# A last RMSNorm whose sums are spread by a matrix of ones, and other banks for the first output tiles, in a hybrid decoder layer

## The chip, the cores and the metric

The kernel runs on one core of a Trainium2 chip. The time is the device time of one execution in microseconds, and a run is judged by the median of several executions. A profiled execution of the kernel before gives the span, the busy times of the engines, and the order of every instruction. TensorE is called PE in the profile (PEld are its weight loads), VectorE is DVE, ScalarE is ACT, GpSimd is POOL, and SP is the engine that issues most of the transfers.

## The reference

The layer takes `x` of 1 x 1024 x 1024 (tokens by channels, f32). Cut to what matters here:

```python
h = rmsnorm(x, norm1_w)
proj = h @ w_in                      # q, k, v, z of mixer A; gates; q, k, v of mixer B
o_a = (rmsnorm(gated_delta_rule(...), gdn_norm_w) * silu(z))      # 4 heads of 128
o_b = dilated_attention(qb, kb, vb)                               # 8 heads of 64
x = x + concat([o_a, o_b]) @ w_out
h = rmsnorm(x, norm2_w)
u = causal_dwconv(h @ w_up, ffn_conv_w)
x = x + (silu(gate) * up) @ w_down
return rmsnorm(x, final_norm_w)      # x * rsqrt(mean(x * x over channels) + 1e-6) * w
```

The last line is the norm that the change rewrites. The product with `w_out` is the output projection, whose banks it exchanges.

## The kernel before

Everything is held transposed: channels on the 128 partitions, tokens along the free dimension. A row of 1024 channels is so eight tiles of 128 partitions, and a norm over channels is a sum over partitions and over eight tiles. Products are made three times with parts of f32 (high by high, low by high, high by low; `mm3`), at the rate of fp32r; a few small ones are plain f32 products.

Python code writes the program. A planner (`Weave`) runs the stages as streams and fixes the order on TensorE; `need` makes a stream wait, in the planner's own model of time, until a tile is ready. On the other engines the framework's scheduler sets the order from the dependencies and from its own simulated timeline; `after(a, b)` adds an order by hand, `keep` chains instructions in the order written. `defer` puts pieces of VectorE's work into a queue from which `background` takes them.

PSUM has eight banks, in four pairs with tags: `hf` (the projection), `asc` (attention's scores and their transposes), `ch` and `atr`. `bank(tag)` takes the next one of a pair, which must have been read out by those who used it last.

The output projection (`out_proj`, line 1328) makes eight tiles of 128 output channels, each in two halves of 512 tokens, summed over k = 0 to 7 (four heads of mixer A, four pairs of heads of mixer B). The first two tiles (`MORDER[0]`, `MORDER[1]`) are made side by side while the last heads are still being split into high and low parts (`ohi`, `olo`): for each k that is done, first the two halves of the one tile, then those of the other. Their banks are taken on line 1358: `hf` for the first, `asc` for the second. All later tiles take `hf` (line 1369). Just before, the stream `dense` has made the last tile of z in the `hf` banks; VectorE reads it out into `xr`. VectorE also finishes the last attention group (`oT`), the gate (`zz`, `og`), and the low parts of the heads (`olo`).

At the end (`mlp_down`, line 1865) the last product is made in pieces. The eight tiles of the result, `x1h[0]` to `x1h[7]`, are complete for the second half of the tokens first; of the first half, the left 256 tokens and then the right 256 are finished. For the last piece the squares of `x1h[4]` and `x1h[5]` are added into `rstdB` with the others, and those of `x1h[6]` and `x1h[7]` are kept alone (`squares`). Then `final_norm(0, right, ("hf", "ch"), more=squares)`, line 1924, does this:

- TensorE multiplies each 128-token block of the three square tiles, as weights, with one column of ones: the sums come out with tokens on partitions, two numbers per partition (`ss`).
- ScalarE takes the root, VectorE the reciprocal, of those two numbers (`rs`).
- Four transposes of `rs`, spread along its free dimension, put one copy of the result on all partitions into a bank (`pb`), and a second copy into another bank (`pb_`).
- ScalarE copies the second one to SBUF (`pbs`), and GpSimd multiplies `x1h[2]` and `x1h[3]` by it; ScalarE has scaled these two by the norm's weight `fw` before.
- VectorE scales the other six tiles by `fw` and `pb` in one instruction each (line 1840), and each tile is stored when it is done, by SP's queue or ScalarE's.

The left part's eight scalings (`outs`) are put around this by hand, lines 1921 to 1923:

```python
        after(outs[1], last["sum"], "the last norm waits for it")
        after(outs[1], adds[2, right.start], "the last norm waits for it")
        after(outs[5], adds[3, right.start], "the last norm waits for it")
```

`adds[3, ...]` is VectorE's addition of the last product to its tile.

Of the kernel before, what the change touches and what calls it, by code (L numbers as in the profile page):

```python
# [7 lines left out]
F32 = mybir.dt.float32  # L8
F32R = mybir.dt.float32r
AF = mybir.ActivationFunctionType  # L10
OP = mybir.AluOpType
# [4 lines left out]
P = 128  # L16
# [134 lines left out]
def hybrid_layer(tc, I, out):  # L151
# [3 lines left out]
    ve = Engine(wv, nc.vector, "vector", 0.07, 0.00105)  # L155
    ac = Engine(wv, nc.scalar, "scalar", 0.12, 0.00085)
# [3 lines left out]
    po_ = Engine(wv, nc.gpsimd, "gpsimd", 0.15, 0.0021)  # L160
    sy = Engine(wv, nc.sync, "sync", 0.05, 0.00142, 2.2)
# [3 lines left out]
    sa = Engine(wv, nc.scalar, "sync", 0.05, 0.00142, 2.2)  # L165
# [4 lines left out]
    sp = es.enter_context(tc.tile_pool(name="sp", bufs=1))  # L170
# [3 lines left out]
    def tile_(pool, shape, dt, name, tag, bufs):  # L174
        return wv.slot(pool.tile(list(shape), dt, name=name, tag=tag, bufs=bufs), tag, bufs)
# [12 lines left out]
    def const(name, shape, src=None):  # L188
        t = cp.tile(list(shape), F32, name=name)
        if src is not None:  # L190
            sy.dma_start(t, src)
        return t
# [3 lines left out]
    def after(inst, anchor, reason="keeps a slot free until it is needed"):  # L196
        tc.add_manual_dep(inst.ins, anchor.ins.name, order, reason=reason)
# [44 lines left out]
    def mm(dst, lhs, rhs, us, start=True, stop=True, **kw):  # L242
        tc.stamp_issue_order_token(nc.tensor.matmul(dst, lhs, rhs, start=start, stop=stop, **kw).ins, TOKEN)  # L243
        wv.product(us, dst, lhs, rhs)

    def tp(dst, src):
        tc.stamp_issue_order_token(nc.tensor.transpose(dst, src, ident).ins, TOKEN)  # L247
        wv.product(0.11, dst, src)
# [45 lines left out]
    eps = const("eps", [P, 1])  # L294
# [26 lines left out]
    def bank(tag, name="ps"):  # L321
        return tile_(pp_, (P, 512), F32, name, tag, 2)
# [40 lines left out]
    for k in range(KT):  # L363
# [11 lines left out]
        if k == 0:  # L375
            sy.dma_start(wst[:, 0, :], I["w0"][0, :, 0])
            for h in range(2):
# [8 lines left out]
                                         op0=OP.mult, op1=OP.subtract)  # L386
# [3 lines left out]
        else:  # L390
            if k % 2 == 0:
                sy.dma_start(wst, I["w0"][k // 2])
            parts = [half(0), half(1)] if k == 1 else [slice(0, S)]
# [14 lines left out]


    ident = const("ident", [P, P], I["ident"])  # L410
    ones = const("ones", [P, 8])
    ve.memset(ones, 1.0)
    tri = tile_(sp, [P, P], F32, "tri", "r0", 1)
    sy.dma_start(tri, I["tri"])
# [41 lines left out]
    rstdB = const("rstdB", [P, S])  # L456
# [834 lines left out]
    last = {}  # L1291
# [34 lines left out]
    fw = const("fw", [P, KT], I["fw"])  # L1326

    def out_proj():
        yield from wv.until("dense")
        kept, pieces[:] = pieces[:], []  # L1330
        made = first_out + [wk(I["wo"][MORDER[1]], None, 4)]
        pieces.extend(kept)
        ws, lows = [t[:2] for t in made], [t[2:] for t in made]
        yield from wv.until("last group")
        yield from wv.until("residual")
        pts, third = {}, []
        todo = [(k, j) for k in range(8) for j in range(2)]
        while todo:

            now = [a for a in todo if ("ot", a[0]) in wv.done and (a[1] == 0 or "attention" in wv.done)]  # L1340
            if not now:
                yield 0.3
                continue
            k, j = now[0]
            todo.remove(now[0])
            m, w = MORDER[j], ws[j]
            last["products"] = True
            for low in lows[j]:
                flush(low)
            if k == H and not third:  # L1350

                third.extend(A(nm, "qa", F32R) for nm in ("whi", "wlo"))
                raw = raw_weight(I["wo"][MORDER[2]])
                ac.activation(third[0], raw, AF.Copy)
                defer(*[(third[1], lambda c=c: ve.tensor_tensor(third[1][:, c], raw[:, c], third[0][:, c].bitcast(F32),
                                                                op=OP.subtract), [third[0]]) for c in quarters])
            if m not in pts:
                pts[m] = [bank(("hf", "asc")[j]) for _ in range(2)]
            for h in range(2):
                yield wv.need(pts[m][h], *w, *ots[k])  # L1360
                mm3(pts[m][h], [t[:, k, :] for t in w], [t[:, half(h)] for t in ots[k]], k == 0, k == 7)
        wv.done.add("firsts")
        for j, m in enumerate(MORDER):
            w = ws.pop(0)
            for h in range(2):
                if j > 1:
                    if j == 2:
                        flush(third[1])
                    pt = bank("hf")
                    yield wv.need(pt, *w)  # L1370
                    for k in range(8):
                        mm3(pt, [t[:, k, :] for t in w], [t[:, half(h)] for t in ots[k]], k == 0, k == 7)
                        yield 0.0
                else:
                    pt = pts[m][h]
                ve.tensor_tensor(x1[m][:, half(h)], x1[m][:, half(h)], pt, op=OP.add)
            if j + 2 < 8:
                ws.append(wk(I["wo"][MORDER[j + 2]]) if j else
                          [t.rearrange("p (k m) -> p k m", k=KT) for t in third])
                load_residual(MORDER[j + 2])  # L1380
            elif j == 6:
                up_first()
                wv.done.add("last weights")
            residual(m)
        wv.done.add("proj")
# [224 lines left out]
    x1h = {}  # L1610
# [160 lines left out]
    def part(m, hh, sl):  # L1771
        return slice(512 * hh + sl.start, 512 * hh + sl.stop)
# [22 lines left out]
            if turn:  # L1795
                keep("vector", inst)

    def final_norm(hh, sl, tags, between=None, more=()):
        n_ = (sl.stop - sl.start) // P
        ss = bank(tags[0])  # L1800
        o = 512 * hh + sl.start
        parts = [rstdB[:, o:o + n_ * P]] + list(more)
        for i, t in enumerate(parts):
            for c in range(n_):
                mm(ss[:, c:c + 1], t[:, c * P:(c + 1) * P], ones[:, :1], 0.215, i == 0 and c == 0,
                   i == len(parts) - 1, skip_group_check=True)
        rs = tile_(sp, [P, 4], F32, "rs3", "rs3", 2)
        if more:
            ac.activation(rs[:, :n_], ss[:, :n_], AF.Sqrt, scale=1.0 / 1024, bias=eps)
            ve.reciprocal(rs[:, :n_], rs[:, :n_])  # L1810
        else:
            inst = ve.tensor_scalar(rs[:, :n_], ss[:, :n_], 1.0 / 1024, EPS, op0=OP.mult, op1=OP.add)
            rsqrt(rs[:, :n_], rs[:, :n_], n_)
        if hh:

            keep("vector", inst)
            rp, rs = rs, tile_(sp, [P, 4], F32, "rs3", "rs3", 2)
            keep("vector", ve.tensor_copy(rs, rp))
        elif between is not None:
            rp, rs = rs, tile_(sp, [P, 4], F32, "rs3", "rs3", 2)  # L1820
            last["mean"] = ve.tensor_copy(rs[:, :n_], rp[:, :n_])
        if between is not None:
            between()
        pb = bank(tags[1])
        for c in range(n_):
            tp(pb[:, c * P:(c + 1) * P], rs[:, c:c + 1].to_broadcast([P, P]))
        insts = []
        if more:

            pb_ = bank(tags[0])  # L1830
            for c in range(n_):
                tp(pb_[:, c * P:(c + 1) * P], rs[:, c:c + 1].to_broadcast([P, P]))
            ps_ = tile_(sp, [P, 256], F32, "pbs", "t2", 2)
            ac.activation(ps_, pb_[:, :n_ * P], AF.Copy)
            for m in (2, 3):
                x = x1h[m][:, part(m, hh, sl)]
                po_.tensor_tensor(x, x, ps_, op=OP.mult)
        for m in (0, 1, 4, 5, 6, 7) if more else range(8):
            x = x1h[m][:, part(m, hh, sl)]
            insts.append(ve.scalar_tensor_tensor(x, x, fw[:, m:m + 1], pb[:, :sl.stop - sl.start], op0=OP.mult, op1=OP.mult))  # L1840
            (sa if more and m in (1, 6) else sy).dma_start(out[m * P:(m + 1) * P, part(m, hh, sl)], x)
            if more and m in (4, 6):

                m = 2 if m == 4 else 3
                sa.dma_start(out[m * P:(m + 1) * P, part(m, hh, sl)], x1h[m][:, part(m, hh, sl)])
        return insts

    def square(m, hh=0):
# [16 lines left out]
    def mlp_down():  # L1865
# [3 lines left out]
        pb = [bank(t, "dw") for t in ("hf", "ch") for _ in range(2)]  # L1869
# [15 lines left out]
        for n, (stage, j) in enumerate(STEPS):  # L1885
# [5 lines left out]
            if (stage, j) == (3, HT - LAST - 2):  # L1891
                outs = final_norm(1, whole, ("hf", "ch"), lambda: down_step(stage, j))
# [7 lines left out]
        adds = {}  # L1900
# [19 lines left out]

        after(outs[1], last["sum"], "the last norm waits for it")
        after(outs[1], adds[2, right.start], "the last norm waits for it")
        after(outs[5], adds[3, right.start], "the last norm waits for it")
        final_norm(0, right, ("hf", "ch"), more=squares)

    wv.add(0, norms())
    wv.add(1, gates())
# [73 lines left out]
```

## Time and profile before

| What | Value |
|---|---|
| median of 3 runs | 1181.21 us (1180.98 to 1181.97) |
| profiled execution, its own time | 1181.01 us |
| its span | 1179.2 us |
| PE busy | 1170.6 us (99%) |
| DVE busy | 948.1 us (80%) |
| ACT busy | 555.5 us (47%) |
| POOL busy | 54.2 us (5%) |
| mean granted clock of TensorE | 0.998 |

The span runs from the first to the last instruction of the execution; the time has a little more around it. In the rows of the timeline the first number is the start in us from the span's start, the second the duration of the row (of all its instructions together, where it ends in x2 or more), then engine, line, operation, output <- inputs, and forms; in brackets stands how long the engine was idle before, and who ended that. In the rows of groups the numbers behind the count are the busy time in us and the mean of one in ns. Most instructions carry the line of a helper (L142 for VectorE, ScalarE and GpSimd, L243 for products, L247 for transposes), so the names of the tiles tell them apart.

### The profile page before, as it was taken

The page shows a single profiled execution, that of the slowest core. Times are in us where ns is not written, and L with a number is a line of the kernel's source. Part 1 is how long each engine was busy: PE and PEld are TensorE (multiplying, and loading weights), DVE is VectorE, ACT ScalarE, POOL GpSimd, SP SyncE. Part 2 cuts the span into 40 slices and gives each one's busy share as a digit, 9 for nine tenths or more (in the row PEclk, how much of TensorE's full clock was granted, in tenths as well). Part 3 has the DMA queues.
Part 4 walks back from the last instruction along what each step waited for, and adds up shares of the span by engine and source line. Part 5 has one row for each costly group of instructions (what it writes and reads, how often), then busy time and mean ns, then how long its engine had stood idle before and what let it go on. Part 6 is the DMA issues. An engine that isn't in the chain of part 4 may idle for free.

```text
span 1179.2 us, 18158 instructions
## 1 busy us (share of the span) xinstructions
PE 1170.6 (99%) x6958; PEld 967.0 (82%) x6958; DVE 948.1 (80%) x1559; ACT 555.5 (47%) x1000; POOL 54.2 (5%) x46
## 2 busy tenths in 40 slices
PE   9999999999999999999999999999999999999997
PEld 7888888898777778888888888888888888888887
DVE  8676997464566677768999898888989889998987
ACT  7473433333334444655545454444444453546452
POOL 0122001003200000000000000000000000000001
PEclk9999999999999999999999999999999999999999
DMA  7424566838564315532231222223131494457734
GB/s 241 109 82 148 146 166 182 260 100 252 183 193 136 126 38 171 196 126 96 83 107 57 104 75 87 93 69 108 54 107 54 150 388 168 131 178 226 233 98 160
DMA packets 122103, 167.48 MB, mean 142 GB/s; under 512 B 55776, under 2 KB 70944, under 8 KB 122016
## 3 DMA queue, kind: packets, MB, share of 16 engines
q1 hardware_dynamic: 121296, 165.80, 43.8%
q8 instruction: 54, 0.88, 0.3%
q10 hardware_dynamic: 720, 0.53, 0.1%
q14 instruction: 33, 0.27, 0.1%
HBM read 126.09 MB, written 40.21 MB: 141 GB/s over the span
## 4 chain that ended last, share of the span: by engine, by line
PE 99%; DVE 1%; ACT 0%; issue 0%; DVEq 0%; ACTq 0%
PE ps L243 48%; PE pa L243 20%; PE dw L243 18%; PE pc L243 10%; PE ps L252 1%; PE ps L247 1%; DVE x1h L142 0%; PE warm L243 0%; PE pd L243 0%; DVE wke L144 0%; ACT w L144 0%; DVE aqkv L142 0%; DVE xr L142 0%; ACT sq L142 0%; DVEq L1997 0%
## 5 line engine op out<-in xcount | busy, mean ns | idle before, releaser
L243 PE MATMUL dw<-pr 128*128 128x512 f32 (+1 forms) x984 | 211.4, 377 | 0.0
L243 PEld LDWEIGHTS dw<-pr 128*128 128x128 f32 x984 | 176.7, 188 | 33.6
L243 PE MATMUL ps<-xhi,whi 128*128 128x512 f32 x448 | 177.0, 409 | 0.0
L243 PE MATMUL ps<-xhi,wlo 128*128 128x512 f32 x448 | 169.5, 391 | 0.0
L243 PE MATMUL ps<-xlo,whi 128*128 128x512 f32 x448 | 169.1, 391 | 0.0
L243 PE MATMUL pa<-T,pair 128*128 128x512 f32 x528 | 126.9, 389 | 0.0
L243 PEld LDWEIGHTS pa<-T,pair 128*128 128x128 f32 x528 | 99.2, 188 | 20.6
L243 PEld LDWEIGHTS ps<-xhi,whi 128*128 128x128 f32 x448 | 84.1, 188 | 18.7 <-issue 2.1
L243 PEld LDWEIGHTS ps<-xhi,wlo 128*128 128x128 f32 x448 | 84.0, 188 | 18.8 <-issue 0.6
L243 PEld LDWEIGHTS ps<-xlo,whi 128*128 128x128 f32 x448 | 84.2, 189 | 15.4 <-DVE xlo L142 0.4
L142 ACT ACTIVATE u<-pa 128x512 f32<-128x512 f32 x44 | 26.4, 599 | 114.4 <-PE pa L243 114.3
L142 DVE SCALAR_TENSOR_TENSOR y<-xu,fcw,y 128x1023 f32<-128x1023 f32 (+1 forms) x44 | 56.4, 1281 | 22.1 <-ACT y L142 22.0
L142 ACT ACTIVATE pr<-wd 128x1024 fp32r<-128x1024 f32 x33 | 35.0, 1061 | 73.6 <-DVE wd L142 38.6
L243 PE MATMUL pa<-B,A 128*128 128x512 f32 x264 | 63.5, 390 | 0.0
L243 PE MATMUL pc<-B,pair 128*128 128x512 f32 x264 | 63.4, 389 | 0.0
L243 PE MATMUL pc<-T,S 128*128 128x512 f32 x264 | 63.4, 389 | 0.0
L243 PE MATMUL pa<-T,S 128*128 128x512 f32 x264 | 63.4, 389 | 0.0
L142 DVE TENSOR_TENSOR wst<-wst 128x512 f32<-128x512 f32 x88 | 60.4, 686 | 0.8
L243 PE MATMUL ps<-B,pair 128*128 128x512 f32 x252 | 60.5, 389 | 0.0
L144 ACT ACTIVATE sm<-sm,mx 128x128 f32<-128x128 f32 (+7 forms) x64 | 35.4, 555 | 51.6 <-DVE mx L144 51.6
L142 DVE TENSOR_TENSOR wlo<-wst,whi 128x256 fp32r<-128x256 f32 (+3 forms) x74 | 47.9, 676 | 13.9 <-ACT whi L142 13.8
L243 PEld LDWEIGHTS pa<-T,S 128*128 128x128 f32 x264 | 49.6, 188 | 10.3
(245 smaller groups left out, 2155.1 us busy)
## 6 DMA issues: line engine op xcount, KB each, us to landing
wst<-in_wu SPq DMA_DIRECT2D x44, 512.0 KB
wd<-in_wd SPq DMA_DIRECT2D x44, 512.0 KB
wst<-in_wi SPq DMA_DIRECT2D x25, 512.0 KB
upark<-y SPq DMA_DIRECT2D x22, 512.0 KB
r<-upark SPq DMA_DIRECT2D x22, 512.0 KB
wa<-in_wd SPq DMA_DIRECT2D x22, 256.0 KB
apark<-aqkv SPq DMA_DIRECT2D x8, 512.0 KB
wst<-in_wo SPq DMA_DIRECT2D x8, 512.0 KB
```

The source lines that it names most:

```text
L142: return getattr(eng, op)(*a, **kw)
L144: inst = getattr(eng, op)(*a, **kw)
L243: tc.stamp_issue_order_token(nc.tensor.matmul(dst, lhs, rhs, start=start, stop=stop, **kw).ins, TOKEN)
L247: tc.stamp_issue_order_token(nc.tensor.transpose(dst, src, ident).ins, TOKEN)
L252: tc.stamp_issue_order_token(nc.tensor.transpose(dst, src[rows], ident[rows, rows]).ins, TOKEN)
```

## The change

The last piece's norm gets a function of its own, `last_norm`. It multiplies the three square tiles, now as the moving operand of 256 columns, with a 128 x 128 matrix of ones as weights: each product puts the sum over partitions on every partition, and the three accumulate in one bank (`ss`, 128 x 256). ScalarE takes the root of all 256 columns into SBUF (`root`), VectorE writes the reciprocal into another bank (`pb`), ScalarE copies that to SBUF for GpSimd (`by`), and the scalings and stores follow as before. The transposes, the small `rs` and the second bank are gone from it; `final_norm` loses the branches for `more`. The tile `ones` grows from 8 to 128 columns. One more of the left part's scalings is put behind the last addition (`outs[4]` in place of `outs[5]`).

In `out_proj`, the first tile takes the `asc` banks and the second the `hf` banks; the third tile takes `asc`, and the others `hf`.

```diff
-    ones = const("ones", [P, 8])
+    ones = const("ones", [P, P])
     ve.memset(ones, 1.0)
...
             if m not in pts:
-                pts[m] = [bank(("hf", "asc")[j]) for _ in range(2)]
+                pts[m] = [bank(("asc", "hf")[j]) for _ in range(2)]
...
-                    pt = bank("hf")
+                    pt = bank("asc" if j == 2 else "hf")
...
-    def final_norm(hh, sl, tags, between=None, more=()):
+    def last_norm(sl, tags, more):
+        n = sl.stop - sl.start
+        ss, pb = bank(tags[0])[:, :n], bank(tags[1])[:, :n]
+        for i, t in enumerate([rstdB[:, sl]] + more):
+            mm(ss, ones, t, 0.43, i == 0, i == len(more))
+        root, by = [tile_(sp, [P, 256], F32, nm, "t2", 2) for nm in ("root", "by")]
+        ac.activation(root, ss, AF.Sqrt, scale=1.0 / 1024, bias=eps)
+        ve.reciprocal(pb, root)
+        ac.activation(by, pb, AF.Copy)
+        def store(m, eng):
+            eng.dma_start(out[m * P:(m + 1) * P, sl], x1h[m][:, sl])
+        for m in (2, 3):
+            po_.tensor_tensor(x1h[m][:, sl], x1h[m][:, sl], by, op=OP.mult)
+        for m in (0, 1, 4, 5, 6, 7):
+            x = x1h[m][:, sl]
+            ve.scalar_tensor_tensor(x, x, fw[:, m:m + 1], pb, op0=OP.mult, op1=OP.mult)
+            store(m, sa if m in (1, 6) else sy)
+            if m in (4, 6):
+                store(2 if m == 4 else 3, sa)
+
+    def final_norm(hh, sl, tags, between=None):
...
-        if more:
-            ac.activation(rs[:, :n_], ss[:, :n_], AF.Sqrt, scale=1.0 / 1024, bias=eps)
-            ve.reciprocal(rs[:, :n_], rs[:, :n_])
-        else:
+        if True:
             inst = ve.tensor_scalar(rs[:, :n_], ss[:, :n_], 1.0 / 1024, EPS, op0=OP.mult, op1=OP.add)
...
-        after(outs[5], adds[3, right.start], "the last norm waits for it")
-        final_norm(0, right, ("hf", "ch"), more=squares)
+        after(outs[4], adds[3, right.start], "the last norm waits for it")
+        last_norm(right, ("hf", "ch"), squares)
```

More of the change, by code (lines that the diff above doesn't have):

```diff
@@ L1801, in final_norm @@
         o = 512 * hh + sl.start
[L1802 to L1806, printed above, removed]
+        for c in range(n_):
+            mm(ss[:, c:c + 1], rstdB[:, o + c * P:o + (c + 1) * P], ones[:, :1], 0.215, c == 0, True,
+               skip_group_check=True)
         rs = tile_(sp, [P, 4], F32, "rs3", "rs3", 2)
-        if more:
-            ac.activation(rs[:, :n_], ss[:, :n_], AF.Sqrt, scale=1.0 / 1024, bias=eps)
-            ve.reciprocal(rs[:, :n_], rs[:, :n_])
-        else:
+        if True:
             inst = ve.tensor_scalar(rs[:, :n_], ss[:, :n_], 1.0 / 1024, EPS, op0=OP.mult, op1=OP.add)
@@ L1827, in final_norm @@
         insts = []
[L1828 to L1838, printed above, removed]
+        for m in range(8):
             x = x1h[m][:, part(m, hh, sl)]
             insts.append(ve.scalar_tensor_tensor(x, x, fw[:, m:m + 1], pb[:, :sl.stop - sl.start], op0=OP.mult, op1=OP.mult))
[L1841 to L1845, printed above, removed]
+            sy.dma_start(out[m * P:(m + 1) * P, part(m, hh, sl)], x)
         return insts
```

## The prediction

> **What bounds the kernel now.** I read the page first, then the timeline of the last stretch, then the groups by form for prices, then the timeline around the output projection, the other place that the diff touches.
>
> ```profile
> span 1179.2 us, 18158 instructions
> PE 1170.6 (99%) x6958; PEld 967.0 (82%) x6958; DVE 948.1 (80%) x1559; ACT 555.5 (47%) x1000; POOL 54.2 (5%) x46
> PE 99%; DVE 1%; ACT 0%; issue 0%; DVEq 0%; ACTq 0%
> ```
>
> TensorE is busy 99% of the span, and the chain that ended last is TensorE up to its last 1%. So an edit counts in two ways only: it takes a hole out of TensorE's stream (and nothing downstream puts it back), or it shortens the chain that is left when the last product is done. The diff tries both: the last norm is that chain, the banks of the first output tile are such a hole. The last stretch, order of time:
>
> ```profile
> 1166.46 3.83 PE L243 MATMUL dw<-pr 128*128 128x256 f32 x30
> 1168.87 1.65 DVE L142 SCALAR_TENSOR_TENSOR x1h<-x1h,fw,ps 128x256 f32<-128x256 f32 x4
> 1170.12 0.50 PE L243 MATMUL ps<-ones,rstdB 128*128 128x1 f32 x4
> 1170.43 0.41 DVE L142 TENSOR_TENSOR x1h<-x1h,dw 128x256 f32<-128x256 f32 x1
> 1170.77 1.26 DVE L142 SCALAR_TENSOR_TENSOR x1h<-x1h,fw,ps 128x256 f32<-128x256 f32 x3
> 1170.94 0.42 ACT L142 ACTIVATE sq<-x1h 128x256 f32<-128x256 f32 x1 [1.48 <-DVE x1h L142]
> 1171.41 0.61 PE L243 MATMUL ps<-ones,sq 128*128 128x1 f32 x4 [0.34 <-ACT sq L142]
> 1172.11 0.26 ACT L142 ACTIVATE rs<-ps,eps 128x2 f32<-128x2 f32 x1 [0.76 <-PE ps L243]
> 1172.41 0.17 DVE L142 RECIPROCAL rs<-rs 128x2 f32<-128x2 f32 x1 [0.39 <-ACT rs L142]
> 1172.72 0.62 PE L247 MATMUL ps<-ident,rs 128*128 128x128 f32 x4 [0.70 <-DVE rs L142]
> 1173.16 2.44 DVE L142 SCALAR_TENSOR_TENSOR x1h<-x1h,fw,ps 128x256 f32<-128x256 f32 x6 [0.59 <-PE ps L247]
> 1173.44 0.38 ACT L142 ACTIVATE pbs<-ps 128x256 f32<-128x256 f32 x1 [1.06 <-PE ps L247]
> 1173.90 1.41 POOL L142 TENSOR_TENSOR x1h<-x1h,pbs 128x256 f32<-128x256 f32 x2 [8.27 <-ACT pbs L142]
> ```
>
> To be seen: a chain in which each link waits for the one before. The last product ends at 1166.46 + 3.83 = 1170.29; the last add runs 1170.43 to 1170.84, its square to 1171.36, the sums over partitions to 1172.02, the root on two numbers per partition to 1172.37, the reciprocal to 1172.58, the transposes that spread it, and the first scaling starts at 1173.16. From there to the end of the span (1179.2) are 6.0 us: six scalings on DVE to 1175.60, with two products on POOL beside them (to 1175.31), and the last stores. This rest keeps its work, so the first scaling's start is the measure of the new norm. Hops between engines, from these rows: DVE to ACT 0.10 (1170.84 to 1170.94), ACT to PE 0.05, PE to ACT 0.09, ACT to DVE 0.04, ACT to POOL 0.08.
>
> **The new norm, step by step.** Removed: four transposes and the spare bank with the second copy of the spread (1172.58 to 1173.16: 0.58 us on the chain). Added: root, reciprocal and sums no longer work on 2 numbers per partition but on 256. Prices:
>
> ```profile
> L142 DVE RECIPROCAL rs<-rs 128x2 f32<-128x2 f32 x1 | 0.2, 165 | 0.4 <-ACT rs L142 0.4
> L142 DVE RECIPROCAL dens<-dens 128x8 f32<-128x8 f32 x8 | 1.5, 193 | 0.0
> L142 DVE RECIPROCAL beta<-beta 128x32 f32<-128x32 f32 x1 | 0.4, 352 | 0.0
> L144 DVE COPY pt<-ps 128x256 f32<-128x256 f32 x56 | 20.1, 417 | 14.9 <-PE ps L252 14.9
> L142 DVE COPY rstdB<-ps 128x512 f32<-128x512 f32 x4 | 2.7, 684 | 0.6 <-PE ps L247 0.6
> L142 ACT ACTIVATE sums<-ps,eps 128x256 f32<-128x256 f32 x1 | 0.5, 474 | 3.1 <-PE ps L243 3.1
> L243 PE MATMUL ps<-rstdB,picks 128*32 128x256 f32 x8 | 0.6, 391 | 0.0
> ```
>
> - Sums. Each f32 product is two passes (two products of one column show x4). A pass of 256 columns takes 0.39 by the picks row, like the 512-column fp32r passes further down, which follow each other in 0.23. The passes over rstdB and the first square (four, from 1170.12) end before the last square comes; the last product takes 0.23 + 0.39 = 0.62 against 0.61 now. Cost nothing, covered by the wait for the square.
> - The add before it. One left scaling is put behind it (the anchor moves from the sixth to the fifth). DVE's four scalings end at 1168.87 + 1.65 = 1170.52 and the add is packed right behind them; without the fourth it starts when the product is there, 1170.29 + 0.04 = 1170.33. Gain 0.10. Four scalings at 0.39 then run behind the add, to about 1172.3, still before the root is there: free.
> - Root. Between the plain copy out of PSUM (0.38, the pbs row) and the scaled one with a bias (0.47, the sums row). It has scale and bias: 0.47, so +0.21.
> - Reciprocal. From 2 to 32 numbers it grows by 187 ns, 6.23 ns each, and the value at 8 (202 by that line, 193 shown) lies on it; a copy grows by (684 − 417) / 256 = 1.04 ns. On 256 numbers: 165 + 254 × 6.23 = 1748 ns, 1.75 us against 0.17. Bounds: 0.42 (an ordinary pass) and 2.28 (the steepest reading, below). I take 1.75: three sizes lie on one line, though the jump from 32 to 256 is wide.
> - The copy for POOL. It reads the bank from which DVE's scalings read. Now there are two banks with the same content, one for each engine. What happens when ScalarE and VectorE read one bank, attention shows:
>
> ```profile
> 441.67 0.75 DVE L144 COPY pt<-ps 128x256 f32<-128x256 f32 x2 [0.45 <-PE ps L252]
> 442.12 0.76 ACT L144 ACTIVATE pb<-ps 128x128 f32<-128x128 f32 x4 [0.26 <-DVE pt L144]
> L144 ACT ACTIVATE pb<-ps 128x128 f32<-128x128 f32 (+3 forms) x64 | 14.4, 268 | 21.6 <-DVE pt L144 15.4 <-issue 5.3
> ```
>
> Both read the same transposes, neither needs the other's result, and yet ScalarE's idle time is ended by VectorE's copy (15.4 of 21.6 us): readers of one bank take turns in the order written. In the new code the copy is written ahead of the scalings, so they wait for it: hop 0.10, copy 0.38, hop 0.04, in all 0.52. Bounds 0 and 0.52; I take 0.52, the row is the same pair of engines.
>
> Sum: add 1170.33 to 1170.74; square 1170.84 to 1171.26; sums 1171.31 to 1171.93; root 1172.02 to 1172.49; reciprocal 1172.53 to 1174.28; copy 1174.38 to 1174.76; first scaling 1174.80 against 1173.16: **1.64 us later**. POOL's two products would end at 1174.76 + 0.08 + 1.41 = 1176.25, before DVE's last scaling (1177.24), as now. The wider memset of ones is free: 128 columns cost what dens costs below, and DVE idles behind the memsets.
>
> ```profile
> L142 DVE MEMSET dens<- 128x128 f32 x1 | 0.2, 165 | 0.0
> 4.01 0.35 DVE L142 TENSOR_SCALAR xhi<-xt,n 128x256 fp32r<-128x256 f32 x1 [2.68 <-DMA xt<-in_xT]
> ```
>
> **The banks.** The first output tile starts when the last z tile's product ends, and its second half needs the bank that this product has just filled:
>
> ```profile
> 445.20 0.42 ACT L144 ACTIVATE pb<-ps 128x128 f32<-128x128 f32 x2
> 449.76 0.76 DVE L142 TENSOR_TENSOR xr<-ps,rstdB 128x256 f32<-128x256 f32 x2 [0.21 <-PE ps L243]
> 449.79 0.39 PE L243 MATMUL ps<-olo,whi 128*128 128x512 f32 x1
> 450.02 0.39 PE L243 MATMUL ps<-ohi,wlo 128*128 128x512 f32 x1
> 450.66 0.47 PE L243 MATMUL ps<-ohi,whi 128*128 128x512 f32 x1 [0.26 <-DVE xr L142]
> 450.97 0.40 PE L243 MATMUL ps<-olo,whi 128*128 128x512 f32 x1
> 453.40 1.06 DVE L142 TENSOR_TENSOR oT<-ps,rB 128x128 f32<-128x128 f32 x4
> 457.21 1.21 DVE L142 TENSOR_TENSOR olo<-og,ohi 128x1024 fp32r<-128x1024 f32 x1
> 458.48 0.19 PEld L243 LDWEIGHTS ps<-olo,whi 128*128 128x128 f32 x1 [0.25 <-DVE olo L142]
> 458.49 0.49 PE L243 MATMUL ps<-olo,whi 128*128 128x512 f32 x1
> ```
>
> Steps are 0.23; here they are 0.64 and 0.31, so the hole is 0.41 + 0.08 = 0.49 us. The scores' banks were read last at 445.62, so with them the hole closes. But 36 products later (six of k = 0 for each of two tiles, likewise k = 1 and 2) TensorE needs the low part of the fourth head, made until 457.21 + 1.21 = 458.42, and already waits 0.25 for its weight load. TensorE 0.49 earlier waits 0.49 longer there: VectorE's queue between 449.76 and 458.42 hangs on the last z product and not on the output tiles. Gain: between 0 and 0.49; I take 0, since the wait that takes it stands in the trace. The second tile in the projection's banks needs the one that xr frees at 450.52 only 12 products in: no wait. The third tile gets the first one's banks as before.
>
> Total +1.64 and 0: span 1180.8. Around the span lie 1181.01 − 1179.2 = 1.8 us, so 1182.65, say **1182.7**. The profiled execution is 0.2 below the median of 1181.21; the range holds both.
>
> **The rivals**, each from 1182.65, and a difference under 0.2% (2.4 us) can hardly be told from no change here.
> - *The hole stays closed* (1182.2): VectorE puts the four oT pieces (1.06 us at 453.40) behind the head's own work, its low part comes a microsecond sooner, and 0.49 is kept. For it: the kernel's planner sees other waits. Against: nothing in VectorE's queue there depends on these banks. 0.17.
> - *No turns at the bank* (1182.1): the scalings start beside the copy, 0.52 sooner. Against it the rows of attention. 0.08.
> - *An ordinary reciprocal*, the side on which it isn't slower: it streams at 0.42 us, 1.33 less, and the change ends at 1181.3, 0.3 over this execution. It decides from about 0.4 down: there the difference (0.3 us) is below the spread of the runs shown, 1180.98 to 1181.97. Against: 352 ns for 32 numbers, which a copy's slope cannot give. 0.07.
> - *A steeper reciprocal* (1183.2): every number holds the pipe for eight of a copy's steps, 8 × 1.04 = 8.3 ns, in all 165 + 254 × 8.3 = 2.28 us, 0.53 more. Against: 6.23 ns from 2 to 32, six steps. 0.12. The Trainium skill (VectorE: DVE Perf Modes, "First, the fixed hardware budget") says that reciprocal is an iterative divide with a repeat count of 8; the three sizes here don't show the eight.
> - *The reciprocal is queued ahead of the four left scalings*: VectorE runs its queue in order, so they come behind it, 1.57 us of which the copy's 0.52 covers a part: +1.05, 1183.7, the one case clearly slower by over 0.2%. It decides if the scheduler expects the root before those four. Against: now the three go ahead of the reciprocal, with 0.39 idle after them. 0.06.
>
> **How the numbers follow.** The main case has 0.47, and 0.03 is left for another order elsewhere. Range 1181.6 to 1183.5: it takes in all but the ordinary reciprocal, the queue case and the unknown, 0.16, with the 0.2 between this execution and the median. Faster by over 0.2% has no case but the unknown: 0.03. Slower by over 0.2% (above 1183.6): the queue case, half of the steep reciprocal with the run's scatter, some of the unknown and of a main case with a dearer hop: 0.18. Within: 0.79.
>
> **What would show it.** In the profile after: a RECIPROCAL of 128x256 at 1.75 us with the copy right behind it and six scalings that wait for ACT, not PE; the first of them 4.5 us after the start of the last add (2.73 now); no 0.64 step at the first output tile, but a weight load that waits about 0.7 for olo some 8 us on. Wrong if the reciprocal is under 1.2 us, if the scalings overlap the copy, or if TensorE's stream after the output projection starts earlier by half a microsecond.

## The result, and the profile after

The changed kernel takes 1186.11 us (median of 5 runs, 1185.21 to 1188.34); the kernel before, run beside it, takes 1181.81 us (median of 5, 1180.98 to 1182.95). The ratio is 1.0037, with a 95% interval of 1.0026 to 1.0049: slower by 4.4 us (3.1 to 5.8). The forecast was 1182.7 us, in a range that ended at 1183.5. The profiled execution of the changed kernel is the longest of its five (1188.34 us), so its trace shows the losses somewhat enlarged. The page of the kernel after, with span, busy times and the shares of the chain that ended last:

```profile
span 1186.5 us, 18135 instructions
PE 1172.9 (99%) x6948; PEld 967.9 (82%) x6948; DVE 948.3 (80%) x1559; ACT 555.7 (47%) x1000; POOL 54.5 (5%) x46
PE 89%; DVE 4%; DMA 3%; SPq 1%; ACT 1%; issue 1%; DVEq 0%; ACTq 0%
```

TensorE is still busy 99%, but the chain is no longer TensorE from end to end: a tenth of it now lies on VectorE, on transfers and on queues, where 1% did before. A longer tail alone could not do that; 10% of the span is over 100 us. The tail itself, in the timeline of the kernel after:

```profile
1171.92 3.83 PE L243 MATMUL dw<-pr 128*128 128x256 f32 x30
1175.79 0.42 DVE L142 TENSOR_TENSOR x1h<-x1h,dw 128x256 f32<-128x256 f32 x1 [0.20 <-PE dw L243]
1176.13 1.65 DVE L142 SCALAR_TENSOR_TENSOR x1h<-x1h,fw,ps 128x256 f32<-128x256 f32 x4
1176.31 0.42 ACT L142 ACTIVATE sq<-x1h 128x256 f32<-128x256 f32 x1 [1.38 <-DVE x1h L142]
1176.77 0.70 PE L243 MATMUL ps<-sq,ones 128*128 128x256 f32 x2 [0.16 <-ACT sq L142]
1177.51 0.47 ACT L142 ACTIVATE root<-ps,eps 128x256 f32<-128x256 f32 x1 [0.79 <-PE ps L243]
1178.02 1.76 DVE L142 RECIPROCAL ps<-root 128x256 f32<-128x256 f32 x1 [0.24 <-ACT root L142]
1179.81 0.39 ACT L142 ACTIVATE by<-ps 128x256 f32<-128x256 f32 x1 [1.83 <-DVE ps L142]
1180.23 2.44 DVE L142 SCALAR_TENSOR_TENSOR x1h<-x1h,fw,ps 128x256 f32<-128x256 f32 x6 [0.45 <-ACT by L142]
```

From the end of the last product (1171.92 + 3.83 = 1175.75) to the first scaling (1180.23) are 4.48 us. Before they were 2.87 (1170.29 to 1173.16), so the norm costs 1.61 us more. The rest stands in the first row: that last product ends 5.46 us later than before. The loss lies upstream, in a part of the program that the diff does not seem to touch. The waits of TensorE name the place, first before, then after:

```profile
PE ps L247 <- DVE rs L142: 0.7, 1, 0.7
PE ps L243 <- ACT sq L142: 0.3, 1, 0.3
PE ps L243 <- DVE xr L142: 0.3, 1, 0.3
```

```profile
PE ps L243 <- ACT x L142: 2.1, 1, 2.1
PE ps L243 <- DVE olo L142: 0.4, 1, 0.4
PE ps L243 <- DVE aqkv L142: 0.4, 1, 0.4
```

The wait for `olo` comes back below, with the banks. Two waits are new: for `aqkv`, VectorE's read-out of the projection, and for `x`, a step of mixer A's delta rule. The timelines around the second wait, ScalarE's row and a window of before (a window has its length, the busy time of PE, PEld, DVE, ACT and POOL, then granted clock, transfer share and GB/s), and then ScalarE's and TensorE's rows and two windows of after:

```profile
216.08 1.06 ACT L142 ACTIVATE whi<-wst 128x1024 fp32r<-128x1024 f32 x1 [5.99 <-DMA wst<-in_wi]
220.00:224.00 4.00, 4.00 (x35) 3.34 (x31) 1.61 (x3) 3.28 (x10) 0.00 (x0) 1.00 1.02 333
```

```profile
220.50 1.06 ACT L142 ACTIVATE whi<-wst 128x1024 fp32r<-128x1024 f32 x1 [8.86 <-DMA wst<-in_wi]
221.59 0.59 ACT L142 ACTIVATE x<-ps 64x512 f32<-64x512 f32 x1
222.23 0.37 PE L243 MATMUL ps<-um,x 64*64 64x64 f32 x1 [2.06 <-ACT x L142]
```

```profile
220.00:224.00 4.00, 1.94 (x35) 1.77 (x35) 2.34 (x3) 1.65 (x2) 0.00 (x0) 0.78 0.93 336
224.00:228.00 4.00, 4.00 (x46) 3.56 (x45) 2.01 (x3) 3.64 (x10) 0.00 (x0) 0.79 1.04 406
```

A weight tile lands 4.4 us later. ScalarE's queue holds its split (`whi`) ahead of the read-out of `x`, and TensorE stands still for 2.06 us until `x` is there. Behind this hole its granted clock is 0.78 and 0.79 as means of two windows of 4 us, where the window of before shows 1.00; a window cut to 222.20 to 225.60 us has 0.50, the next one 1.00 again. That costs another 1.5 us in this execution, by the starts of the same products in both traces. In all, the stream falls back by 4.3 us from 192 us until then. A further 0.9 us is lost in the first 8 us; that amount was -0.2 to 0.7 in the other profiled executions, whatever the kernel, and isn't laid to the change.

What the two waits have in common with the diff is one number: the tile `ones` is 480 bytes longer per partition, and every tile that is allocated behind it starts 480 bytes further on. Before, the large tiles start at multiples of 512 bytes; after, each starts 224 bytes past a multiple of 256. The theory to be tested was that this placement slows the transfers. Its rivals were that the new norm or the other banks move the planner's order upstream, or that the weights' staging tiles matter and not those of mixer A.

### The profile page after: what moved, and what is told of

Its sections match the earlier page's. It is cut to its first block, busy times and chain, and to the rows that moved or that the text cites. A ratio compares the mean times of both kernels' runs of the same rounds, so it can differ in the third digit from the quotient of the medians.

```text
span 1186.5 us, 18135 instructions
## 1 busy us (share of the span) xinstructions
PE 1172.9 (99%) x6948; PEld 967.9 (82%) x6948; DVE 948.3 (80%) x1559; ACT 555.7 (47%) x1000; POOL 54.5 (5%) x46
## 4 chain that ended last, share of the span: by engine, by line
PE 89%; DVE 4%; DMA 3%; SPq 1%; ACT 1%; issue 1%; DVEq 0%; ACTq 0%
PE ps L243 39%; PE pa L243 20%; PE dw L243 18%; PE pc L243 10%; SPq L142 1%; DVE vT L142 1%; PE ps L252 1%; DMA vdram<-vT 1%; DMA vtok<-vdram 1%; DVE at L142 1%; ACT vtok L142 1%; PE ps L247 0%; DMA wst<-in_wi 0%; ACT whi L142 0%; DMA qd<-gamdram 0%
## 5 line engine op out<-in xcount | busy, mean ns | idle before, releaser
L142 ACT ACTIVATE whi<-wst 128x1024 fp32r<-128x1024 f32 (+2 forms) x38 | 38.4, 1009 | 42.5 <-PE ps L243 26.6
```

Of the source, the lines that this page charges most:

```text
L142: return getattr(eng, op)(*a, **kw)
```

## The experiments

Ratios are against the kernel before, run beside it on the same chip (medians 1181.78 to 1181.79 us); 0.0010 is 1.2 us.

**Only the wide ones** (`wide_ones`):

```diff
-    ones = const("ones", [P, 8])
+    ones = const("ones", [P, P])
```

> The kernel before, with the constant ones 128 columns wide and nothing else changed: every working tile moves up by 480 bytes in its partition, off the multiples of 512 where it lay. Placement theory (transfers take longer at the new addresses): 2 to 3 us slower than before (1.0018 to 1.0025), transfer packets about 2.5% longer in sum, first queue's share near 44.6%, and TensorE's stream late before the output projection starts. Norm theory (the change's loss is all in the last norm and its banks): no difference, below 0.5 us. Scatter theory (clock and transfers differ from execution to execution): no difference between the medians.

Measured: 1185.52 us, 1.0029 [1.0019, 1.0038]. One number in the kernel before, with no instruction added, makes 3.4 us of the 4.4, more than the 2 to 3 expected. The forecast that all packets together take 2.5% longer did not come: the first queue's share is 43.8% in both traces. Nor is the engines' own work longer: VectorE is busy 948.1 us before and 948.2 here, ScalarE 555.5 and 555.4. Where the loss comes from shows on ScalarE, which scales each head's tokens (`vtok`) when they are back from DRAM. First three heads of before, then of this kernel:

```profile
130.78 2.45 ACT L142 ACTIVATE vtok<-vtok,nk 128x128 f32<-128x128 f32 x8
155.95 2.46 ACT L142 ACTIVATE vtok<-vtok,nk 128x128 f32<-128x128 f32 x8 [0.82 <-DMA vtok<-vdram]
180.82 2.44 ACT L142 ACTIVATE vtok<-vtok,nk 128x128 f32<-128x128 f32 x8 [1.44 <-DMA vtok<-vdram]
```

```profile
131.92 2.45 ACT L142 ACTIVATE vtok<-vtok,nk 128x128 f32<-128x128 f32 x8 [1.15 <-DMA vtok<-vdram]
158.32 2.45 ACT L142 ACTIVATE vtok<-vtok,nk 128x128 f32<-128x128 f32 x8 [2.51 <-DMA vtok<-vdram]
183.68 2.45 ACT L142 ACTIVATE vtok<-vtok,nk 128x128 f32<-128x128 f32 x8 [2.48 <-DMA vtok<-vdram]
```

The work takes as long as before (2.45 us), but it starts 1.1, then 2.4, then 2.9 us later, each time because the transfer has not landed. VectorE's queue follows it; before, and then in this kernel with GpSimd's and TensorE's row:

```profile
188.66 1.27 DVE L142 SCALAR_TENSOR_TENSOR vT<-xr,gcw,vT 128x1022 f32<-128x1022 f32 x1
189.85 1.11 DVE L142 TENSOR_TENSOR aqkv<-ps,rstdB 128x512 f32<-128x512 f32 x1
```

```profile
191.06 2.40 POOL L142 TENSOR_TENSOR qd<-qd,qT 128x1024 f32<-128x1024 f32 x1 [3.42 <-DMA x<-xdram]
191.52 3.02 DVE L142 SCALAR_TENSOR_TENSOR vT<-xr,gcw,vT 128x1022 f32<-128x1022 f32 x1
194.46 1.03 DVE L142 TENSOR_TENSOR aqkv<-ps,rstdB 128x512 f32<-128x512 f32 x1
195.63 0.47 PE L243 MATMUL ps<-xhi,whi 128*128 128x512 f32 x1 [2.37 <-DVE aqkv L142]
```

VectorE comes to the filter `vT` 2.86 us late, and there it runs into GpSimd's product, which costs 1.75 more (3.02 against 1.27). The read-out that frees TensorE's bank is then 4.6 us late: more than the slack of before, and the last 2.37 us of it is a hole in TensorE's stream. Behind it the clock falls as in the kernel after (0.51 from 195.9 to 199.3 us), which costs 1.6 us more. In the kernel after itself the filter starts ahead of GpSimd's product (191.86 and 192.32 us) and takes 1.27; the wait for `aqkv` is only 0.4 there, and the large hole comes later. The Trainium skill (SBUF — State Buffer, "SBUF: two separate sides") says that VectorE with two SBUF inputs and GpSimd share one port pair, which one of them locks for a whole instruction; the trace agrees, as `vT` ends 1.08 us (its own length is 1.27) after GpSimd does at 193.46.

**The change with its tiles back in place** (`after_pad`, against the kernel after):

```diff
-    ones = const("ones", [P, P])
+    ones = const("ones", [P, P + 8])
...
-            mm(ss, ones, t, 0.43, i == 0, i == len(more))
+            mm(ss, ones[:, :P], t, 0.43, i == 0, i == len(more))
```

> The kernel after, with ones 136 columns wide (the product uses 128): the working tiles lie 512 bytes higher than before, on multiples of 512 again. Placement theory: only the norm's own loss is left, 1.6 us over before (1.0014). Norm and scatter theories: as the kernel after, 4.3 us over before (1.0037).

Measured: 1183.27 us, 1.0012 [1.0003, 1.0021]: 1.4 us (0.4 to 2.5) slower than before, and 0.0025 under the kernel after's ratio. The new norm is there in full, with the first add at 1170.99 and the first scaling 4.44 us behind it, as in the kernel after:

```profile
1170.99 0.42 DVE L142 TENSOR_TENSOR x1h<-x1h,dw 128x256 f32<-128x256 f32 x1 [0.20 <-PE dw L243]
1173.21 1.76 DVE L142 RECIPROCAL ps<-root 128x256 f32<-128x256 f32 x1 [0.24 <-ACT root L142]
1175.01 0.38 ACT L142 ACTIVATE by<-ps 128x256 f32<-128x256 f32 x1 [1.83 <-DVE ps L142]
```

The waits for `aqkv` and `x` are gone from TensorE's list. Neither the new norm nor the new banks opens them. The traces of before and after agree with that: by the names of their tiles, TensorE's first 6942 products stand in the same order in both, and the other engines' instructions do so up to the last norm. The planner's order did not move.

**Only the banks** (`swap_only`): the kernel before with the exchange of `asc` and `hf` in `out_proj` as in the diff.

> The kernel before with the exchanged banks alone. Prediction's step: the 0.49 us hole at the first output tile closes and the wait for olo of the fourth head grows by as much: 0 us, median within 0.4 us of before. Rival (the hole stays closed): 0.5 us faster. Bank theory (the exchange costs somewhere else): 2 us slower or more.

Measured: 1182.19 us, 1.0001 [0.9992, 1.0010]. The trace has both halves of the forecast, TensorE's hole at the first output tile gone and a longer wait at the fourth head's low part:

```profile
450.57 0.39 PE L243 MATMUL ps<-ohi,wlo 128*128 128x512 f32 x1
450.79 0.39 PE L243 MATMUL ps<-ohi,whi 128*128 128x512 f32 x1
458.95 0.19 PEld L243 LDWEIGHTS ps<-olo,whi 128*128 128x128 f32 x1 [0.71 <-DVE olo L142]
```

The step of 0.64 is 0.22 now, and the weight load waits 0.71 us where it waited 0.25. By the starts of the same products, each of the five kernels with the new banks gains 0.52 to 0.53 us at the first output tile. Two single waits don't show that `olo` takes it back, because this wait differs from one profiled execution to the next: 0.18 to 0.83 us in the seven kernels with the old banks (mean 0.57), 0.71 to 1.19 in the four with the new banks and the old order of `olo` (`swap_only`, `after`, `after_pad`, `sbuf_recip`; mean 0.98). The means differ by 0.40, about what was gained. The time alone (0.9 us faster to 1.2 slower) leaves out neither 0 nor the rival's 0.5 us.

**Other offsets** (`plus32`, `plus64`, `plus256`): the kernel before with `ones` of 16, 24 and 72 columns, so that all tiles behind it start 32, 64 and 256 bytes further on.

```diff
-    ones = const("ones", [P, 8])
+    ones = const("ones", [P, 16])      # plus32; 24 in plus64, 72 in plus256
```

> The kernel before with ones 16 columns wide: the working tiles lie 32 bytes off the multiples of 512. Placement theory, if any offset hurts: 2 to 3 us slower, as with 480 bytes. If it is the end of the tile or the amount of the shift that counts: no difference.

> The kernel before with ones 24 columns wide: the working tiles lie 64 bytes off the multiples of 512. If what counts is a start at a multiple of 256 bytes (the Trainium skill, DMA: Bandwidth & Descriptors, How a descriptor splits into AXI transactions, lets a descriptor that starts off 256 bytes take a further transaction): slow like the offsets of 32 and 480, 2.5 to 3.5 us over before (about 1.0025). If a multiple of 64 suffices: no difference.

> The kernel before with ones 72 columns wide: the working tiles lie 256 bytes off the multiples of 512. With a grain of 256 bytes: no difference to before, packets as short as before. With a grain of 512: 2.5 to 3.5 us slower.

Measured: 1184.96 us, 1.0027 [1.0017, 1.0038] at 32 bytes; 1183.52 us, 1.0015 [1.0006, 1.0024] at 64; 1181.62 us, 0.9999 [0.9991, 1.0008] at 256. So neither the size of `ones` nor the distance moved counts, but the place in a grain of 256 bytes (or of 128, which no run has). The longest wait of TensorE for `aqkv` is 2.3 us at 32 and 2.2 at 64, and there is none at 256. That 64 bytes cost less than 32, and less than the 2.5 to 3.5 us expected, stays unexplained; the intervals overlap.

**Which tiles** (`weights_off`, `chain_off`): an unused tile moves the one group or the other. In `weights_off` the constants and the staging tiles of the weights (`wst`) start 32 bytes off and all tiles behind them are back on multiples of 512; in `chain_off` it is the other way round.

```diff
-    ones = const("ones", [P, 8])                              # weights_off
+    ones = const("ones", [P, 16])
...
+    ve.memset(wp.tile([P, 120], F32, name="offset"), 0.0)     # [P, 8] in chain_off, ones as before
```

> The other half: the staging tiles of the weights lie 32 bytes off, all tiles behind them on multiples of 512 (again one memset more). If the loss comes from the round trips of the delta rule: under 1 us. If from the weight loads: 2 to 3 us.

> The kernel before with an unused tile of 32 bytes among the weight tiles (one small memset more on VectorE at the start): the staging tiles of the weights (wst) stay on multiples of 512, everything behind them lies 32 bytes off, the delta rule's tiles with their round trips through DRAM included. If the loss comes from those round trips: nearly all of it is here, 2 to 3 us. If from the weight loads: under 1 us.

Measured: `weights_off` 1182.13 us, 1.0002 [0.9993, 1.0011]; `chain_off` 1185.30 us, 1.0030 [1.0019, 1.0042]. The whole loss is with the tiles behind the staging tiles. ScalarE's waits for `vtok` from 120 to 225 us (total, times, longest) in `weights_off`, and in `chain_off` with TensorE's new wait:

```profile
ACT vtok L142 <- DMA vtok<-vdram: 2.8, 3, 1.4
```

```profile
ACT vtok L142 <- DMA vtok<-vdram: 5.2, 3, 2.5
PE ps L243 <- DVE aqkv L142: 1.8, 1, 1.8
```

Each packet's duration is in the traces too. Means over all 45,696 packets of 128 bytes (most belong to the round trips of mixer A through DRAM, 16,384 to mixer B's `avt`) and over the 2,048 of 1024 bytes (output stores of 256 columns), worked out from the packets' records:

| Kernel | Offset from a multiple of 256 | 128 B, ns | 1024 B, ns | Ratio |
|---|---|---|---|---|
| before | 0 | 12.1 | 45.9 | |
| plus256 | 0 | 12.1 | 45.9 | 0.9999 |
| weights_off | 0, staging tiles 32 | 12.1 | 45.9 | 1.0002 |
| after_pad | 0 | 12.1 | 45.9 | 1.0012 (new norm and banks) |
| plus32 | 32 | 13.0 | 46.8 | 1.0027 |
| chain_off | 32, staging tiles 0 | 13.0 | 46.9 | 1.0030 |
| plus64 | 64 | 13.2 | 46.9 | 1.0015 |
| wide_ones | 224 | 13.6 | 49.1 | 1.0029 |
| after | 224 | 13.6 | 49.2 | 1.0037 (new norm and banks) |

The packets fall into two classes as the times do; inside the slow class they don't follow the times (`plus64`). The same records show the step to `vtok`: from the first packet's start to the last one's end, the write of a head's `vT` to DRAM (4,096 packets) takes 2.97 to 3.01 us for the first two heads in all seven kernels at offset 0, and 3.84 to 4.12 in all five at 32, 64 and 224. One more microsecond per head stands against the first `vtok` of `wide_ones` that is 1.1 us late. The large packets (2048 and 4096 bytes, the weights' among them) keep their median, 84 and 159 ns, in every kernel, which fits that `weights_off` loses nothing. The Trainium skill (DMA: Bandwidth & Descriptors, "How a descriptor splits into AXI transactions") says that an access starts at the 256-byte boundary at or below its first byte and pays for what lies between in beats of 32 bytes. An estimate from that page, for 128-byte packets that start in turn at 0 and 128 bytes of a tile's row: 6 beats each on the mean at offset 0, 7 at 32, 8 at 64, 9 at 224. The packets' order agrees (12.1, 13.0, 13.2, 13.6 ns), the amounts are smaller.

**The reciprocal into SBUF** (`sbuf_recip`, against `after_pad`): no bank for two readers, and no copy.

```diff
-        ve.reciprocal(pb, root)
-        ac.activation(by, pb, AF.Copy)
+        ve.reciprocal(by, root)
...
-            ve.scalar_tensor_tensor(x, x, fw[:, m:m + 1], pb, op0=OP.mult, op1=OP.mult)
+            ve.scalar_tensor_tensor(x, x, fw[:, m:m + 1], by, op0=OP.mult, op1=OP.mult)
```

> The kernel after with its tiles on multiples of 512 (as after_pad), and the reciprocal written to SBUF, from where both VectorE's scalings and GpSimd's products read it: no copy by ScalarE, no bank that two engines read. Turns theory (the scalings wait for ScalarE's copy because both read one bank): the first scaling starts right behind the reciprocal, 0.45 to 0.55 us sooner after it than in after_pad, and the whole is about 1.1 us over before (1.0010). If the scalings did not wait for the copy but for something else: as after_pad, 1.4 to 1.6 us over before.

Measured: 1183.77 us, 1.0016 [1.0007, 1.0025]. Its tail:

```profile
1172.98 1.75 DVE L142 RECIPROCAL by<-root 128x256 f32<-128x256 f32 x1 [0.24 <-ACT root L142]
1174.77 3.49 DVE L142 SCALAR_TENSOR_TENSOR x1h<-x1h,fw,by 128x256 f32<-128x256 f32 x6
1174.81 1.59 POOL L142 TENSOR_TENSOR x1h<-x1h,by 128x256 f32<-128x256 f32 x2 [8.76 <-DVE by L142]
```

The scalings now start 0.04 us behind the reciprocal instead of 0.45 (1178.02 + 1.76 to 1180.23 in the kernel after): the turns at the bank are real and cost 0.41. But six scalings take 3.49 us where they took 2.44, because all their inputs now lie in SBUF and GpSimd works beside them: one by one, the two scalings that meet GpSimd's products (until 1176.40) take 1.05 and 0.94 us, and the four after them 0.47 each, as with an input in PSUM. That is 1.05 given back against 0.41 won. So the turns theory holds for the wait, but its total of 1.1 us over before did not come (1.9 measured, 0.8 to 3.0); the run can't tell the total from `after_pad`.

**The hole closed for good** (`hole_closed`): the kernel before with its own norm, the new banks, the fourth head's low part last, and `outs[4]` behind the last addition.

```diff
+            if k == H - 1:
+                for a, b in ((0, 0), (1, 0), (0, 1)):
+                    for h in range(2):
+                        yield wv.need(pts[m][h], w[a], ots[k][b])
+                        mm(pts[m][h], w[a][:, k, :], ots[k][b][:, half(h)], 0.2135, False, False)
+                continue
```

> The kernel before with the exchanged banks, and for the fourth head (k = 3) the products that need its low part put behind the other four of the tile; one left scaling more behind the last add, as in the change; the last norm and the placement of before. Prediction's step: the hole of 0.49 us closes and the wait for olo, now asked for 0.7 us later, takes back 0 to 0.1 of it: 0.4 to 0.6 us faster than before (0.9995 to 0.9997), and TensorE's stream behind the output projection that much earlier relative to its start. If the wait just grows again: no difference.

Measured: 1180.90 us, 0.9993 [0.9984, 1.0002]. That can't be told from no change. In the trace the parts are there: TensorE gains 0.53 us at the first output tile and loses 0.06 of it at `olo`, by the starts of its products. The weight load for `olo` waits 0.34 and not 0.71, and at the end the first scaling starts at 1172.89 against 1173.16:

```profile
458.99 0.30 PEld L243 LDWEIGHTS ps<-olo,whi 128*128 128x128 f32 x2 [0.34 <-DVE olo L142]
1170.15 0.42 DVE L142 TENSOR_TENSOR x1h<-x1h,dw 128x256 f32<-128x256 f32 x1 [0.20 <-PE dw L243]
1172.89 1.26 DVE L142 SCALAR_TENSOR_TENSOR x1h<-x1h,fw,ps 128x256 f32<-128x256 f32 x3 [0.59 <-PE ps L247]
```

## Why the prediction was wrong, and where it was right

**The step that failed** is one sentence of the norm's part: "The wider memset of ones is free". The instruction is free; the tile is not. The prediction costed the edit as an instruction on VectorE and left out that a longer constant moves the address of everything allocated behind it. `wide_ones` measures that term alone: 1.0029, 3.4 us (2.2 to 4.5), more than twice the whole forecast change. Part of it is the clock: the two of its nine executions with a mean clock of 0.998 took 1184.20 and 1184.25 us, the four with 0.996 took 1185.47 to 1186.79; none of the 27 executions of before beside it had 0.996. `plus256` and `after_pad` take it away with a wide tile still there, and `chain_off` against `weights_off` shows which tiles carry it. None of the named rivals was this one; the 0.03 for "another order elsewhere" meant something else, as the order of the instructions is unchanged upstream.

**The sum otherwise held.** Placement 0.0029 (`wide_ones`) and norm with banks 0.0012 (`after_pad`) make 0.0041 against 0.0037 [0.0026, 0.0049]. Without the placement the kernel takes 1183.27 us beside a before of 1181.78, so +1.5 by the medians for the forecast +1.6.

- Norm: 1.61 us from the last product to the first scaling, forecast 1.64; from the add 4.44 us, forecast 4.47.
- Reciprocal: 1.76 us, forecast 1.75. The line through 2, 8 and 32 numbers reaches 256. The rivals of 0.42 and 2.28 us fall, and with the second the count of 8 that the Trainium skill gives for it (VectorE: DVE Perf Modes, "First, the fixed hardware budget"), if a count is a copy's step.
- Root 0.47 as forecast; sums 0.70 for 0.62.
- Turns at the bank: the copy comes first and the scalings wait 0.45 us, forecast 0.52. `sbuf_recip` confirms them, as the scalings then wait 0.04. That rival falls.
- The left scalings went ahead of the reciprocal (1176.13), so the queue rival falls.
- Banks: the hole closes (0.53 us, forecast 0.49), and the wait named grows on the mean of the traces, from 0.57 to 0.98 us. That `swap_only` meets "about 0.7" so exactly is luck: the forecast took 0.25 from one trace, the second shortest of seven. The kernel after shows 0.85. That the gain is 0, and not a few tenths, is within the scatter and not shown.

**How the profile held a warning.** The prediction said that an edit counts only through holes in TensorE's stream or through the last chain, and that was right. It then looked for holes only where the diff has instructions. The profile of before already had ScalarE waiting 0.82 and 1.44 us for `vtok` at 155 and 180 us: round trips with little left to hide them, exposed to anything that touches all transfers.

**What stays open.** The link from longer packets to late `vtok` is read from the traces; no run changed the packets at a fixed placement. The write of `vT` grows by a third where its packets grow by a tenth, and no run says why. Whether 64 bytes really cost less than 32, and how much the reads of a round trip add, stays open too. The wait for `x` behind the weight tile in the kernel after was seen in one profiled execution; its other four runs have no trace.

## What to carry to other kernels

A constant that grows moves every tile behind it: compare the addresses before and after an edit, and pad to a multiple of 256 bytes where small packets go to and from these tiles. A term that costs no instruction can still be the largest in the sum, so ask of each edited allocation what lies behind it, and look for waits in the old profile that are nearly or barely hidden. Putting a value in SBUF to avoid turns at a bank can cost more than the turns if GpSimd reads SBUF at the same time.

## What the runs showed of the hardware that was not expected

- A start of 32, 64 or 224 bytes past a multiple of 256 lengthens 128-byte packets from 12.1 to 13.0, 13.2 and 13.6 ns, and 1024-byte packets from 45.9 to 46.8, 46.9 and 49.1; a shift by 256 does nothing.
- TensorE's granted clock falls to about one half for 3.4 us behind a hole of 2.06 us in the kernel after (0.50) and of 2.37 in `wide_ones` (0.51), but stays at 1.00 behind 2.31 in `plus32` and 2.19 in `plus64`. The length of the hole alone does not decide. The same two windows, in `wide_ones` and then in `plus32`:

```profile
192.00:197.00 5.00, 2.63 (x10) 1.89 (x9) 4.59 (x3) 1.37 (x2) 1.46 (x1) 0.90 0.54 86
197.00:213.00 16.00, 16.00 (x365) 13.24 (x365) 8.28 (x10) 3.88 (x7) 0.00 (x0) 0.93 0.71 167
```

```profile
192.00:197.00 5.00, 2.69 (x12) 1.92 (x12) 4.84 (x3) 1.12 (x2) 1.72 (x1) 1.00 0.55 87
197.00:213.00 16.00, 16.00 (x370) 13.40 (x369) 8.74 (x10) 4.76 (x9) 0.35 (x2) 1.00 0.71 168
```

- A scaling of 128x256 on VectorE takes 0.94 to 1.05 us with all inputs in SBUF while GpSimd works on SBUF, and 0.47 to 0.48 when it does not or when one input is in PSUM. Six of them beside two GpSimd products take 3.49 us in the first case and 2.44 with one input in PSUM.
